# Output projection of a hybrid attention block: w_out loaded and split once per group, and the second half's parts made beside the first half's projection

## The chip, the cores and the metric

The kernel runs on one core of a Trainium2 chip. The core has engines that work on their own and wait for each other by semaphores: TensorE (PE in the profile; its weight loads are PEld), VectorE (DVE), ScalarE (ACT), GpSimd (POOL) and SyncE (SP), whose queue issues most of the DMAs. The metric is the time of one execution on the device in microseconds (us); lower is better.

## The reference

One layer of a decoder for 1024 tokens of width 1024, in float32:

```python
h    = rmsnorm(x, attn_norm_w)
proj = h @ w_in                      # 1024 x 3072: q, k, v of two groups of 8 heads, head size 64
o_dil = dilated_attention(rope(norm(qa)), rope(norm(ka)), va)   # group A: windows 128/512/2048, strides 1/4/16
o_sb  = stick_breaking(qs, ksb, vs)  # group B: sigmoid breaks, reversed cumulative product, strictly causal
mixed = concat(rmsnorm(o_dil, dil_out_norm_w), rmsnorm(o_sb, sb_out_norm_w))   # 1024 x (512 + 512)
x = x + mixed @ w_out                # w_out: 1024 x 1024
h = rmsnorm(x, ffn_norm_w)
x = x + (silu(h @ w_gate) * (h @ w_up)) @ w_down                # inner width 2816
```

The change concerns the line `x = x + mixed @ w_out` and what prepares it. In the kernel group A (dilated) is group 0 and group B (stick-breaking) is group 1. The factor 1/rms of a token is the same for all 512 columns of its group, so the kernel multiplies the group's output by the norm weights first, projects it, and multiplies the result by the factor while adding it to x.

## The kernel before, in words

**Products in three parts.** Each float32 matrix product is made of three faster ones: both operands are split into a high half (a copy on ACT into the reduced type) and a low half (the difference, on DVE or POOL), and `mm3` (lines 91 to 96) sums high x high, high x low and low x high. So each operand of a product costs one ACT pass and one DVE pass first.

**Stages.** First x is normalised and projected for the dilated group. Then eight head pairs follow one another: pairs 1 to 4 are the dilated heads (`attend_a`), pairs 5 to 8 the stick-breaking heads (`attend_b`). In a stick-breaking pair, for each block of 128 queries and each of two heads: scores on PE (L442 to L445, up to two chunks of 512 keys), two sigmoids on ACT per chunk (L564, tiles kp and pb), a scan over the keys on DVE (L567), a product (L568, on POOL for the first head and on DVE for the second), then transposes on PE (L586, tile pt), their evacuation on ACT (L588, tile th) and the product with v (L595, tile pv). After the eight pairs come the feed-forward layers, which are long rows of products from PE.

**The background.** While the pairs run, a generator, `ahead` (line 783), makes other work bit by bit: the projections of the stick-breaking heads, and then group 0's output projection. Every step of it yields a cost in units. The loop over pairs (lines 819 to 836) takes steps as long as the units spent are below a limit that grows with the pair's progress: at pair 8 the limit is 134 + 18 x f, with f the share of the pair that is done. It is only looked at where `attend_b` yields; in pair 8 these limits are 134.1, 134.4, 138.4, 138.8, 139.2, 140.0, 140.6, 141.3, 143.2, 144.0, 145.0 (the last score block), 147.9 and 152.0. What is left after that is traced behind the pair. Each piece of background work is held behind the score matmul that was traced last (`hold`, line 86, and `gate`), so it can't run earlier than that. The projections take 124.8 units, the parts of group 0's first half 0.8, so its output projection starts at 125.6; each of its eight products of 128 tokens by 512 columns takes 2.6 units, half of the tokens 20.8.

**The output projection.** It is made in four quarters (group g, half hf of the tokens: 512 each):
- `merge_parts` (line 745) goes through the four 128-column slices of a group's output: it loads the slice (`load_o`, line 699, from HBM into one of two staging tiles, tag qr), and `out_parts` (line 684) makes its high half on ACT (L688), its low half on DVE (L689), its square on ACT (L693, L696), and adds the squares up on POOL (L697). Four steps, 0.2 units each.
- `load_wout(g, dh)` (line 714) loads the 512 rows of w_out of group g and the left or right 512 columns (dh 0 or 1) in four pieces of 256 KB (L718, three raw tiles, tag wraw) and splits each: copy on ACT (L725), difference on DVE (L726). The left half of group 0 goes to the tiles of the projection weights, all others to tiles of the tags qs and kh, of which there are four each and of which each head pair uses two.
- `merge` (line 753) makes the factor from the summed squares (`out_rstd`, line 704) and then, for each column half and each 128 tokens, `wout` (line 732): twelve matmuls (L92, L95, L96, tile yo) and an addition on DVE (L741).

Group 0's first half is done in `ahead` beside pairs 7 and 8; its weights come in four calls, since the right half is loaded in the middle of the left half's products, and both are loaded again for the second half. Then the parts of the second half are made (146.4 to 147.2 units) and projected. Group 1 follows behind pair 8 (lines 840 to 848), its second half among the first norms of the feed-forward part (lines 882 to 887), with weights loaded anew.

**The order.** A planner at build time fixes the order in which each engine works: it simulates the program with its own durations and, where several instructions could go, takes the one traced earlier. `after` (line 81) adds an order without a wait between engines. The low halves of group 1's w_out and parts are tied behind the last product of the last pair (`last_mul`). On the chip each engine works through its fixed order; one that waits holds up all behind it. SP's queue of DMAs does so too.

Of the kernel before, what the change touches and what calls it, by code (L numbers as in the profile page):

```python
# [32 lines left out]
def f(ap):  # L33
    return ap.bitcast(F32)
# [3 lines left out]
def tile_hybrid_block(ctx, tc, x, attn_norm_w, w_in, q_norm_w, k_norm_w, dil_w, sb_w,  # L38
# [5 lines left out]
    def H(name, dtype=FR):  # L44
        return big.tile([128, 4, 512], dtype, tag="H", name=name, bufs=8)
# [35 lines left out]
    def after(i, first, why, cls=mybir.DependencyClass.NoSync):  # L81

        tc.add_manual_dep(i.ins, first.ins.name,
                          mybir.DependencyInfo(cls, mybir.DependencyReason.DATA), reason=why)
# [6 lines left out]
    def mm3(ps, a, b, first, last, held=False):  # L91
        i = nc.tensor.matmul(ps, a[0], b[0], start=first, stop=False)  # L92
        if first or held:
            hold(i)
        nc.tensor.matmul(ps, a[0], b[1], start=False, stop=False)  # L95
        return nc.tensor.matmul(ps, a[1], b[0], start=False, stop=last)  # L96
# [35 lines left out]
    def P4(name, tag="P"):  # L132
        return att.tile([128, 1024], F32, tag=tag, name=name, bufs={"P": 6, "G": 2, "E": 2, "M": 1}[tag])
# [66 lines left out]
    for tb in range(NT):  # L200
# [15 lines left out]
        t = att.tile([128, 512], F32, tag="rq", name="rq", bufs=2)  # L216
# [20 lines left out]
    for nm, w in (("q", q_norm_w), ("k", k_norm_w)):  # L237
        t = P4("rope" + nm, "E").rearrange("p (s t e) -> p s t e", s=2, t=NT)
# [67 lines left out]
    def project_ahead(i, which, spare=False):  # L306

        if which < 2:
            d = raws[i, which] = dram.tile([128, 1024], F32, name="raw%d%d" % (i, which))
            lows[i, which] = dram.tile([128, 1024], F32, name="low%d%d" % (i, which))  # L310

        def done(hf, p):
            c = slice(hf * 512, hf * 512 + 512)
            if which == 2:
                t = att.tile([128, 512], F32, tag="rq", name="rq", bufs=2)
                nc.scalar.activation(t, p, AF.Copy)
                turns.append(lambda: by_tokens(t, i, hf))
            else:
                h = att.tile([128, 512], FR, tag="rq", name="rh", bufs=2)
                l = att.tile([128, 512], FR, tag="rl", name="rl", bufs=3)  # L320
                split(h, l, p)
                nc.sync.dma_start(d[:, c], f(h))
                nc.sync.dma_start(lows[i, which][:, c], f(l))
                ready.add((i, which, hf))
        wt = weights(1536 + which * 512 + 128 * i, spare)
        return [project(wt, hf, done) for hf in range(2)]
# [357 lines left out]
    def out_parts(g, i, hf, o, parts, acc):  # L684

        w = ow[:, 4 * g + i:4 * g + i + 1]
        h, l = parts[hf][0][:, i, :], parts[hf][1][:, i, :]
        hold(nc.scalar.activation(h, o, AF.Copy, scale=w))  # L688
        j = nc.vector.scalar_tensor_tensor(l, o, w, f(h), op0=ALU.mult, op1=ALU.subtract)  # L689
        if g:  # L690
            after(j, last_mul[0], "the last pair goes first")
        if i == 0:
            hold(nc.scalar.activation(acc[hf], o, AF.Square))  # L693
        else:
            sq = att.tile([128, 512], F32, tag="rt", name="sq", bufs=3)
            hold(nc.scalar.activation(sq, o, AF.Square))  # L696
            nc.gpsimd.tensor_tensor(acc[hf], acc[hf], sq, op=ALU.add)  # L697

    def load_o(g, i, hf):
        t = att.tile([128, 512], F32, tag="qr", name="o", bufs=2)  # L700
        nc.sync.dma_start(t, (oa, ob)[g][i][:, hf * 512:hf * 512 + 512])
        return t

    def out_rstd(g, hf, acc):

        ssp = PS.tile([128, 4], F32, "d", "ssp")
        for k in range(4):
            nc.tensor.matmul(ssp[:, k:k + 1], acc[hf][:, k * 128:(k + 1) * 128], ones, start=True, stop=True)
        r = big.tile([128, 4], F32, name="rg%d%d" % (g, hf))
        nc.vector.tensor_scalar(r, ssp, 1.0 / 512, EPS, op0=ALU.mult, op1=ALU.add)  # L710
        nc.gpsimd.tensor_tensor(r, r, mhalf[:, :4], op=ALU.pow)
        return r

    def load_wout(g, dh):
        wts = []
        for i in range(4):
            raw = big.tile([128, 512], F32, tag="wraw", name="raw", bufs=3)
            nc.sync.dma_start(raw, w_out[g * 512 + i * 128:g * 512 + (i + 1) * 128, dh * 512:dh * 512 + 512])  # L718
            if g or dh:
                t = att.tile([128, 1024], FR, tag=("qs", "kh")[i // 2], name="wo", bufs=4)  # L720
                h, l = t[:, :512], t[:, 512:]
            else:

                h, l = ((att if i == 3 else big).tile([128, 512], FR, tag="rl" if i == 3 else tag, name="wo", bufs=3) for tag in ("wh", "wl"))
            nc.scalar.activation(h, raw, AF.Copy)  # L725
            j = nc.vector.tensor_tensor(l, raw, f(h), op=ALU.subtract)  # L726
            if g:
                after(j, last_mul[0], "the last pair goes first")
            wts.append((h, l))
        return wts  # L730

    def wout(tb, dh, r, parts, wts, tag):
        p = PS.tile([128, 512], F32, tag, "yo")
        c = slice((tb % 4) * 128, (tb % 4) * 128 + 128)
        for i in range(4):
            h, l = parts[tb // 4]
            mm3(p, (h[:, i, c], l[:, i, c]), wts[i], i == 0, i == 3, True)
            if i < 3:
                yield 0.65
        xx = x2[tb // 2][:, 2 * (tb % 2) + dh, :]  # L740
        nc.vector.scalar_tensor_tensor(xx, p, r[:, tb % 4:tb % 4 + 1], xx, op0=ALU.mult, op1=ALU.add)  # L741

    ahead_w = []

    def merge_parts(g, hf, parts, acc):
        o = load_o(g, 0, hf)
        for i in range(4):
            nxt = None if i == 3 else cur.ot[hf] if g and i == 2 else load_o(g, i + 1, hf)
            out_parts(g, i, hf, o, parts, acc)
            o = nxt  # L750
            yield 0.2

    def merge(g, hf, parts, acc):

        r = out_rstd(g, hf, acc)
        if g and hf:
            wts = [load_wout(g, dh) for dh in range(2)]
            for tb in range(4, 8):
                for dh in range(2):
                    for _ in wout(tb, dh, r, parts, wts[dh], ("d", "s")[tb % 2]):  # L760
                        pass
            return
        for dh in range(2):
            wts = ahead_w.pop() if ahead_w else load_wout(g, dh)
            for tb in range(4 * hf, 4 * hf + 4):
                yield from wout(tb, dh, r, parts, wts, "d")
                if g == 0 and tb % 4 == 1 and hf + dh < 2:
                    ahead_w.append(load_wout(g, 1 - dh))
                yield 0.65

    def merge_half(hf):
# [11 lines left out]
    def ahead():  # L783
        for i in range(3):
            for which in (1, 0, 2):
                for part in project_ahead(i, which):
                    yield from part
        for part in project_ahead(3, 1):
            yield from part

        q, v = project_ahead(3, 0), project_ahead(3, 2, True)
        yield from q[0]
        yield from v[0]
        parts, acc = [merge_half(0)], []
        acc.extend(att.tile([128, 512], F32, tag="acc", name="acc", bufs=2) for _ in range(2))
        yield from merge_parts(0, 0, parts, acc)
        yield from q[1]
        yield from v[1]
        while turns:
            turns.pop(0)()  # L800
        yield from merge(0, 0, parts, acc)
        parts.append(merge_half(1))
        yield from merge_parts(0, 1, parts, acc)
        yield from merge(0, 1, parts, acc)

    rest = ahead()
    spent = [0.0]

# [31 lines left out]
    parts = [[H("oh"), H("ol")] for hf in range(2)]  # L840
    acc = [att.tile([128, 512], F32, tag="acc", name="acc", bufs=2) for _ in range(2)]
    for _ in merge_parts(1, 0, parts, acc):
        pass
    for _ in merge(1, 0, parts, acc):
        pass
    parts_1 = merge_parts(1, 1, parts, acc)
    for _ in range(3):
# [18 lines left out]
    for key, tags in (("b11", "PPPP"), ("b21", "PPvv")):  # L866
        t = [att.tile([128, 2, 512], FR, tag=tag, name=key, bufs=BUFS[tag]) for tag in tags]
# [15 lines left out]
        norm2(tb)  # L883
    for _ in parts_1:
        pass
    for _ in merge(1, 1, parts, acc):
        pass
    st = [H("b12", F32), H("b22", F32)]
    for tb in range(4, 8):
# [60 lines left out]
    g = [None] * NF  # L950
# [131 lines left out]
    for k, ft in enumerate(range(NF - LATE, NF)):  # L1082
        r = room[k // 2] if k < 4 else None
# [28 lines left out]
    for hf in range(2):  # L1112
        for ft in list(range(HF, NF - LATE)) + list(range(12 - LATE, HF)):
            c = slice(512 * hf, 512 * hf + 512)
# [5 lines left out]
    for tag, n in (("k2", 2), ("k2", 2), ("kh", 4)):  # L1120
        t = att.tile([128, 1024], F32, tag=tag, name="lk", bufs=n)
# [134 lines left out]
```

## Time and profile before

| | |
|---|---|
| time, median of 3 runs | 1290.96 us (1290.93 to 1292.22) |
| the profiled execution | 1290.87 us, of which span 1288.7 us |
| mean granted clock of TensorE | 0.997 |
| PE busy | 1258.6 us, 98% of the span |
| DVE, ACT, POOL busy | 64%, 47%, 30% |
| bytes moved by DMA | 180.98 MB |
| products of the output projection (tile yo) | 384 matmuls, first start 469.6, last 631.0 us |
| loads and splits of w_out | 32 of each, copies from 441.6 to 611.2 us |
| pair 8's score matmuls | from about 491 to 533 us |

The profile names an instruction by its line, engine, operation and tiles (written <- read). The page gives totals; the same for chosen stretches are windows; the timeline lists instructions in order, equal neighbours merged into one row with their count, and in brackets how long the engine stood idle before a row and what ended that. Matmuls overlap each other a little, so durations of neighbours are longer than the distance of their starts.

### The profile page before, as it was taken

Reading aid. Unit: us, or ns where it says so; the run is one execution under the profiler, and the core shown is the slowest. Engines: PE = TensorE matmul, PEld = TensorE weight load, DVE = VectorE, ACT = ScalarE, POOL = GpSimd, SP = SyncE. Lnnn points to the kernel's source line nnn. Section 1 sums busy time; section 2 is a strip of 40 time slices with the busy share of each in tenths; the row PEclk is TensorE's granted clock in tenths of the full one; section 3 lists DMA queues with packets and bytes.
Section 4 is the critical chain, followed back from the end, with each engine's and each line's share of the span. In section 5 each row is a group of like instructions: output and inputs, shape, how many; then the busy total and the mean of one; then the engine's idle time right before and its main releaser. Section 6 shows DMA issues by size and latency. Waiting matters only on the chain.

```text
span 1288.7 us, 18344 instructions
## 1 busy us (share of the span) xinstructions
PE 1258.6 (98%) x6260; PEld 994.5 (77%) x6260; DVE 830.8 (64%) x1413; ACT 606.0 (47%) x1273; POOL 380.4 (30%) x346
## 2 busy tenths in 40 slices
PE   8999999999999999789999999999999999999998
PEld 6888887777767777568888888888888887878886
DVE  5334356655576867926797677665546876797686
ACT  5431267776686877825473222323332223434442
POOL 2488723353433421312112223212212321010000
PEclk9999999999999999999999999999999999999999
DMA  9633143556646552213256544323445458530352
GB/s 264 238 115 114 49 144 97 150 134 169 168 126 187 190 172 74 82 57 99 66 175 209 172 147 148 113 68 110 144 147 180 137 173 286 161 134 11 130 179 98
DMA packets 198029, 180.98 MB, mean 140 GB/s; under 512 B 33584, under 2 KB 142384, under 8 KB 197936
## 3 DMA queue, kind: packets, MB, share of 16 engines
q1 hardware_dynamic: 195760, 173.39, 43.6%
q0 software_dynamic: 2176, 6.42, 1.8%
q8 instruction: 49, 0.80, 0.3%
q14 instruction: 44, 0.36, 0.1%
HBM read 138.15 MB, written 41.62 MB: 139 GB/s over the span
## 4 chain that ended last, share of the span: by engine, by line
PE 84%; DMA 6%; DVE 4%; ACT 3%; issue 2%; POOL 1%; SPq 0%; DVEq 0%; POOLq 0%; ACTq 0%
PE yd L1156 14%; PE gu L95 11%; PE gu L96 11%; PE gu L92 11%; PE va L96 3%; PE va L92 3%; PE va L95 3%; PE pp L92 3%; PE pp L95 3%; PE pp L96 3%; PE pv L595 2%; PE yo L92 2%; PE yo L96 2%; PE yo L95 2%; PE pt L586 2%
## 5 line engine op out<-in xcount | busy, mean ns | idle before, releaser
L916 ACT ACTIVATE wh<-wr 128x512 fp32r<-128x512 f32 x132 | 83.4, 632 | 211.9 <-PE gu L95 171.7
L95 PE MATMUL gu<-t,wh 128*128 128x512 f32 x352 | 139.0, 395 | 0.0
L92 PE MATMUL gu<-t,wh 128*128 128x512 f32 x352 | 138.8, 394 | 0.0
L96 PE MATMUL gu<-t,wl 128*128 128x512 f32 x352 | 138.8, 394 | 0.0
L1156 PE MATMUL yd<-dl,dh 128*128 128x512 f32 x308 | 122.2, 397 | 2.4 <-DVE dl L917 1.4
L1156 PE MATMUL yd<-dh,dl 128*128 128x512 f32 x308 | 121.1, 393 | 0.0
L95 PE MATMUL gu<-b,wh 128*128 128x512 f32 x264 | 104.5, 396 | 0.0
L92 PE MATMUL gu<-b,wh 128*128 128x512 f32 x264 | 104.3, 396 | 0.0
L96 PE MATMUL gu<-b,wl 128*128 128x512 f32 x264 | 104.2, 396 | 0.0
L567 DVE TENSOR_TENSOR_SCAN kp<-kp,aside 128x640 f32<-128x640 f32 (+7 forms) x56 | 79.0, 1422 | 32.7 <-ACT kp L564 32.6
L1156 PE MATMUL yd<-dh 128*128 128x512 f32 x308 | 85.0, 395 | 0.0
L917 DVE TENSOR_TENSOR wl<-wr,wh 128x512 fp32r<-128x512 f32 x105 | 79.6, 758 | 7.8 <-ACT wh L916 7.8
L92 PEld LDWEIGHTS gu<-t,wh 128*128 128x128 f32 x352 | 66.2, 188 | 15.8
L95 PEld LDWEIGHTS gu<-t,wh 128*128 128x128 f32 x352 | 66.2, 188 | 15.7
L96 PEld LDWEIGHTS gu<-t,wl 128*128 128x128 f32 x352 | 66.1, 188 | 15.7
L92 PE MATMUL pp<-hh,wh 128*128 128x512 f32 x192 | 78.0, 406 | 0.0
L916 ACT ACTIVATE dh<-wd 128x512 fp32r<-128x512 f32 x55 | 34.8, 632 | 89.9 <-PE yd L1156 81.6
L92 PE MATMUL va<-wt,hh 128*128 128x512 f32 x192 | 76.4, 401 | 0.6 <-ACT hh L63 0.5
L96 PE MATMUL va<-wt,hl 128*128 128x512 f32 x192 | 75.9, 398 | 0.9 <-DVE hl L64 0.7
L95 PE MATMUL va<-wt,hh 128*128 128x512 f32 x192 | 75.7, 397 | 0.2 <-DVE wt L154 0.2
L96 PE MATMUL pp<-hh,wl 128*128 128x512 f32 x192 | 75.6, 394 | 0.0
L95 PE MATMUL pp<-hl,wh 128*128 128x512 f32 x192 | 75.6, 394 | 0.0
(216 smaller groups left out, 3025.4 us busy)
## 6 DMA issues: line engine op xcount, KB each, us to landing
wd<-in_w_down_dram SPq DMA_DIRECT2D x88, 256.0 KB, 2.8
wr<-in_w_gate_dram SPq DMA_DIRECT2D x80, 256.0 KB, 3.0
wr<-in_w_up_dram SPq DMA_DIRECT2D x60, 256.0 KB, 3.0
raw<-in_w_in_dram SPq DMA_DIRECT2D x48, 256.0 KB, 4.7
raw<-in_w_out_dram SPq DMA_DIRECT2D x32, 256.0 KB, 2.7
g<-gu SPq DMA_DIRECT2D x20, 256.0 KB, 5.4
xt<-in_x_dram SPq DMA_DIRECT2D x8, 512.0 KB, 7.1
qk<-qr SPq DMA_DIRECT2D x16, 256.0 KB, 2.0
```

The costliest lines, as they stand in the source:

```text
L92: i = nc.tensor.matmul(ps, a[0], b[0], start=first, stop=False)
L95: nc.tensor.matmul(ps, a[0], b[1], start=False, stop=False)
L96: return nc.tensor.matmul(ps, a[1], b[0], start=False, stop=last)
L567: nc.vector.tensor_tensor_scan(rv, rv, (aside[0] if aside[0] is not None else zero)[:, 0:1].to_broadcast([128, n]), 1.0, op0=ALU.mult, op1 ...
L586: i = nc.tensor.transpose(pt[:, c:c + 128], pq[k][s][:, j * 128:(j + 1) * 128], ident)
L595: i = nc.tensor.matmul(pr.pv[64 * s:64 * s + 64, c - n:c], pr.v[:, j, 64 * s:64 * s + 64], th[:, n * s:n * s + n], start=j == 0, stop=j == ...
L916: nc.scalar.activation(h, r, AF.Copy)
L917: i = two(n).tensor_tensor(l, r, f(h), op=ALU.subtract)
L1156: mm = nc.tensor.matmul(pp[k], a[x][:, c], b[y], start=not more and j == order[0] and x + y == 0, stop=j == order[-1] and x == 1, skip_gro ...
```

## The change

`load_wout` becomes a generator: it traces one of its four pieces at each step and hands out the list of tiles, which grows. Both column halves of group 0 are loaded once, ahead of the first half's products: the left half whole and the first piece of the right; the other pieces of the right are traced one after each of the left half's four products. The tiles are kept for the second half of the tokens. In the same way one step of `merge_parts(0, 1)` is traced after each of the first half's four products of the right columns. For group 1 both column halves are loaded ahead of its first half's products and kept for its second half. The x tiles and part tiles of group 0's second half (`merge_half(1)`) are allocated ahead of the first half's products.

```diff
     def load_wout(g, dh):
         wts = []
         for i in range(4):
...
             wts.append((h, l))
-        return wts
+            yield wts
...
-    ahead_w = []
-
...
+    def step(*others):
+
+        for t in others:
+            next(t, None)
+
-    def merge(g, hf, parts, acc):
+    def merge(g, hf, parts, acc, wts, beside=None):
 
         r = out_rstd(g, hf, acc)
         if g and hf:
-            wts = [load_wout(g, dh) for dh in range(2)]
             for tb in range(4, 8):
                 for dh in range(2):
                     for _ in wout(tb, dh, r, parts, wts[dh], ("d", "s")[tb % 2]):
                         pass
             return
         for dh in range(2):
-            wts = ahead_w.pop() if ahead_w else load_wout(g, dh)
             for tb in range(4 * hf, 4 * hf + 4):
-                yield from wout(tb, dh, r, parts, wts, "d")
-                if g == 0 and tb % 4 == 1 and hf + dh < 2:
-                    ahead_w.append(load_wout(g, 1 - dh))
+                yield from wout(tb, dh, r, parts, wts[dh], "d")
+                if beside is not None:
+                    step(beside[dh])
                 yield 0.65
...
-        yield from merge(0, 0, parts, acc)
+        loads = [load_wout(0, dh) for dh in range(2)]
+        wts = [next(t) for t in loads]
+        for _ in loads[0]:
+            pass
         parts.append(merge_half(1))
-        yield from merge_parts(0, 1, parts, acc)
-        yield from merge(0, 1, parts, acc)
+        yield from merge(0, 0, parts, acc, wts, (loads[1], merge_parts(0, 1, parts, acc)))
+        yield from merge(0, 1, parts, acc, wts)
...
-    for _ in merge(1, 0, parts, acc):
+    loads = [load_wout(1, dh) for dh in range(2)]
+    wts = [[a, b, c, d][-1] for a, b, c, d in loads]
+    for _ in merge(1, 0, parts, acc, wts):
         pass
...
-    for _ in merge(1, 1, parts, acc):
+    for _ in merge(1, 1, parts, acc, wts):
         pass
```

The number of matmuls doesn't change. The four steps of `merge_parts(0, 1)` no longer count in the background's units, so the second half's projection starts at 146.4 units instead of 147.2; the steps themselves fall at 137.95, 140.55, 143.15 and 145.75.

## The prediction

> **What bounds the kernel now.** The page's first part comes first, then the same table by windows. In the windows the columns are stretch and length, then busy time with instruction count of PE, its weight loads, DVE, ACT and POOL, then granted clock, DMA share and GB/s.
>
> ```profile
> PE 1258.6 (98%) x6260; PEld 994.5 (77%) x6260; DVE 830.8 (64%) x1413; ACT 606.0 (47%) x1273; POOL 380.4 (30%) x346
> ```
>
> ```profile
> 500.00:520.00 20.00, 20.00 (x143) 14.50 (x142) 11.94 (x13) 14.98 (x34) 3.27 (x3) 1.00 0.13 41
> 520.00:535.00 15.00, 14.61 (x81) 10.61 (x81) 13.56 (x11) 13.05 (x30) 3.32 (x2) 1.00 0.15 51
> 535.00:540.00 5.00, 2.49 (x17) 1.36 (x15) 4.95 (x5) 5.00 (x11) 4.23 (x2) 1.00 0.44 138
> 540.00:545.00 5.00, 1.06 (x4) 0.66 (x5) 4.90 (x4) 3.64 (x7) 2.60 (x2) 0.69 0.40 130
> 545.00:550.00 5.00, 5.00 (x26) 3.46 (x25) 3.88 (x6) 1.35 (x4) 0.14 (x1) 0.63 0.71 224
> 550.00:555.00 5.00, 4.53 (x27) 3.11 (x26) 1.57 (x3) 2.86 (x6) 2.23 (x2) 1.00 0.55 199
> 555.00:560.00 5.00, 2.11 (x10) 1.37 (x8) 1.41 (x2) 3.17 (x7) 2.90 (x4) 1.00 0.16 54
> 560.00:565.00 5.00, 4.87 (x27) 3.58 (x28) 0.75 (x1) 1.44 (x4) 0.94 (x1) 1.00 0.00 0
> 565.00:660.00 95.00, 94.94 (x454) 77.34 (x453) 65.30 (x100) 44.76 (x85) 15.86 (x23) 1.00 0.25 78
> ```
>
> TensorE is busy for 98% of the span, so work taken from another engine is worth nothing wherever PE stays full. The change touches 440 to 631 us. There PE is full up to 520 and again from 565 on, and idle in one place: between 535 and 565 its busy times add to 20.06 of 30 us, 9.94 us idle, and for ten of them the clock is below full. I call this hole the tail: the end of the eighth head pair. What the change is worth has to come from there. The timeline of PE shows what each gap waited for (in brackets: idle before the row, and its releaser):
>
> ```profile
> 526.79 1.03 PE L586 MATMUL pt<-ident,pb 128*128 128x128 f32 x8
> 527.75 1.08 PE L595 MATMUL pv<-th,v 128*64 128x256 f32 x8
> ...
> 532.72 0.50 PE L442 MATMUL sc<-kh,qs 128*128 128x512 f32 x1 [0.36 <-ACT pb L564]
> ...
> 537.71 0.66 PE L586 MATMUL pt<-ident,pb 128*128 128x128 f32 x4 [0.87 <-POOL pb L568]
> 543.47 0.69 PE L586 MATMUL pt<-ident,pb 128*128 128x128 f32 x2 [5.11 <-DVE pb L568]
> 544.63 1.97 PE L586 MATMUL pt<-ident,pb 128*128 128x128 f32 x8 [0.47 <-ACT th L588]
> 546.53 1.98 PE L595 MATMUL pv<-th,v 128*64 128x256 f32 x8
> ...
> 552.23 0.66 PE L586 MATMUL pt<-ident,pb 128*128 128x128 f32 x4 [0.47 <-ACT th L588]
> ...
> 560.13 0.93 PE L586 MATMUL pt<-ident,pb 128*128 128x128 f32 x6 [3.02 <-ACT th L588]
> ```
>
> The gaps are 0.87, 5.11, 0.47, 0.47 and 3.02 us, together 9.94. The largest waits for the last product of the second head (L568 on DVE). Now the two engines that feed it, ACT and then DVE:
>
> ```profile
> 534.20 0.81 ACT L688 ACTIVATE oh<-o,ow 128x512 fp32r<-128x512 f32 x1
> 534.82 0.72 ACT L693 ACTIVATE acc<-o 128x512 f32<-128x512 f32 x1
> 535.34 0.81 ACT L688 ACTIVATE oh<-o,ow 128x512 fp32r<-128x512 f32 x1
> 535.95 0.71 ACT L696 ACTIVATE sq<-o 128x512 f32<-128x512 f32 x1
> 536.47 0.71 ACT L725 ACTIVATE wo<-raw 128x512 fp32r<-128x512 f32 x1
> 536.99 0.67 ACT L564 ACTIVATE kp<-sc 128x512 f32<-128x512 f32 x1
> ...
> 537.95 1.24 ACT L725 ACTIVATE wo<-raw 128x512 fp32r<-128x512 f32 x2
> ...
> 558.96 0.63 ACT L696 ACTIVATE sq<-o 128x512 f32<-128x512 f32 x1 [1.83 <-DMA o<-ob]
> 559.50 1.07 ACT L588 ACTIVATE th<-pt 128x512 f32<-128x512 f32 x2
> ```
>
> ```profile
> 532.65 2.28 DVE L567 TENSOR_TENSOR_SCAN kp<-kp,aside 128x1024 f32<-128x1024 f32 x1
> 535.05 0.75 DVE L689 SCALAR_TENSOR_TENSOR ol<-o,ow,oh 128x512 fp32r<-128x512 f32 x1
> 535.72 0.74 DVE L741 SCALAR_TENSOR_TENSOR x<-yo,rg,x 128x512 f32<-128x512 f32 x1
> 536.38 1.82 DVE L689 SCALAR_TENSOR_TENSOR ol<-o,ow,oh 128x512 fp32r<-128x512 f32 x1
> 538.12 1.76 DVE L726 TENSOR_TENSOR wo<-raw,wo 128x512 fp32r<-128x512 f32 x1
> 539.81 2.27 DVE L567 TENSOR_TENSOR_SCAN kp<-kp,aside 128x1024 f32<-128x1024 f32 x1
> 542.18 1.23 DVE L568 TENSOR_TENSOR pb<-pb,kp 128x1023 f32<-128x1023 f32 x1
> ```
>
> The last score chunk is on PE at 532.72. On ACT five pieces of output work come before its kp, from 534.20 to 536.99: two parts of the dilated second half with their squares, and a copy of w_out. DVE ends its first scan at about 534.9 and starts the second at 539.81, with two low halves, one addition and one w_out split between. So the hole is made by the very work that the change moves or removes, and PE has no other products there, because the second half's projection waits for the same parts.
>
> **The change part by part.** *Loads and splits.* w_out is loaded in 256 KB pieces, 32 before (the page's raw<-in_w_out_dram row) and 16 after: four calls of four pieces instead of eight.
>
> ```profile
> L725 ACT ACTIVATE wo<-raw x32: 615/634/724, 441.6 to 611.2; 128x512 fp32r<-128x512 f32 x32
> L726 DVE TENSOR_TENSOR wo<-raw,wo x32: 654/684/2157, 444.6 to 612.6; 128x512 fp32r<-128x512 f32 x32
> ```
>
> That removes 16 copies of 0.634 us on ACT (10.1 us) and 16 splits of 0.684 us on DVE (10.9 us). Of the four removed calls, the second load of (group 0, left) stood at about 492 to 500, inside full PE: worth 0. The two of group 1's second half stood at 591 to 612, inside the stretch in which PE has 94.94 of 95 us: 0, covered by the projection itself. Only the second load of (group 0, right), at 528 to 538, stands in the tail. Its last copy (536.47) and split (538.12) are two of the intruders; it is priced below with them.
>
> Two rows for the next point, from DVE and from ACT: a projection tile's addition every 0.75 + 2.06 = 2.81 us, and the copies of group 1's right half.
>
> ```profile
> 575.41 0.75 DVE L741 SCALAR_TENSOR_TENSOR x<-yo,rg,x 128x512 f32<-128x512 f32 x1 [2.06 <-PE yo L96]
> ```
>
> ```profile
> 578.92 2.03 ACT L725 ACTIVATE wo<-raw 128x512 fp32r<-128x512 f32 x3 [11.50 <-PE yo L96]
> ```
>
> *The tiles that are held longer.* Both right-column loads use the four tiles that head pairs use. Pair 8 has taken its own two of each tag before the first call, and group 0's right load waits for pair 7's scores as before. Group 1's right load took its tiles at 578.9 us, when PE finished the last left-over product of group 0, and will again; its user comes four products (4 x 2.81 = 11 us) later. Price 0; without that cover it is that wait, a rival below.
>
> *The parts moved.* By the background's budget (the section on the kernel has its numbers) the dilated second half starts at 146.4 units, so all four of its steps are traced at the yield of pair 8 with limit 147.9, held behind the last score matmul: that is the 534.20 above. After, the steps fall at 137.95, 140.55, 143.15 and 145.75, so at the yields with limits 138.4, 140.6, 143.2 and 147.9. Three steps go to about 495 to 525, and only the fourth stays behind the last score. Moved with each step: two ACT passes, one DVE low half, one POOL addition and the next load on SP. There PE has 20.00 of 20 us, DVE 8 and ACT 5 us free: 0 as long as pair 8's own chain has slack there, and as a bound 3 x (0.81 + 0.72) on ACT + 3 x 0.75 on DVE = 6.8 us if none.
>
> *What that gives the tail.* (1) With one step instead of two and no w_out copy, ACT's last kp starts near 535.3 at worst (534.20 plus the 1.14 us between rows 534.20 and 535.34), and the second scan near 536 to 537 instead of 539.81: 3 to 4 us earlier. The rest of the 5.11 us can be filled by products of the second half, of which three quarters can now run, 2.81 us a tile. I take all 5.11; the bounds are 0 and 5.11. (2) Without that gap the clock doesn't fall: eight transposes took 1.97 us instead of 1.03 and eight pv products 1.98 instead of 1.08. That is 0.94 + 0.90 = 1.84 us; bounds 0 and 1.84, I take 1.8. (3) The 0.87 us wait on POOL: half, 0.4. (4) The gaps 0.47, 0.47 and 3.02 us wait for ACT, which stood behind a load of the other group's output (558.96). Those loads can start earlier, since the two staging tiles come free earlier, but the order is still planned and ACT still works in order: bounds 0 and 3.96, I take 1.5. (5) New friction in pair 8, between 0 and the 6.8 above: 0.6, near the low end, since PE was full there with DVE 40% free.
>
> On (2), the Trainium skill, "TensorE: Matmul & The Clock Gate", Part 1, says that PE falls to half clock after about 3.4 us without work and needs as much busy time to come back. The trace agrees: the gap of 5.11 us is followed by 0.63, the gap of 3.02 us leaves 1.00. By that rule a remnant under 3.4 us would cost no clock, which is the 1.8 I took.
>
> Sum: 5.1 + 1.8 + 0.4 + 1.5 - 0.6 = 8.2 us. The profiled execution took 1290.87 us (span 1288.7 and 2.2 around it), 0.09 under the median of the runs. 1290.87 - 8.2 = 1282.7; on the median, **1282.8**. From 565 us on PE is full, so the gain should arrive whole at the end.
>
> **The rivals.** *A, the hole is filled with other work (0.16).* The planner orders each engine by its own durations. With staging tiles free, group 1's copies and squares can slide in front of the last kp, five passes again. For it: in the old order group 1's first copies stand right behind it, at 537.95. Against: group 1's DVE halves are tied behind the last L568, so only ACT is delayed. The 5.11 us gap then stays near 3.5 us, the clock is mostly saved, nothing else is: 1290.9 - 1.6 - 1.4 = 1287.9.
>
> *B, the change doesn't do what it says (0.10).* The parts are ready, but PE's order keeps the transposes in front, and ACT, 13.05 of 15 us busy from 520 and 5.00 of 5 from 535, is itself the limit. Then the hole moves and hardly shrinks: 1290.9 - 1 = 1289.9.
>
> The row for rival C, the POOL additions:
>
> ```profile
> L697 POOL TENSOR_TENSOR acc<-acc,sq x12: 1262/1295/1727, 440.6 to 589.0; 128x512 f32<-128x512 f32 x12
> ```
>
> *C, slower (0.10).* The moved steps wait in ACT's queue of pair 8. Each of its last two needs a load that is issued only when a staging tile is free, and ACT stood 1.83 us before such a load at 558.96. Behind it stand the sigmoids and evacuations that PE needs. Two such waits, 3.7 us, the 6.8 us bound of the passes, and three POOL additions of 1.30 us that hold up DVE passes, 3.9 us, are 14.4 us; against a tail that still gains the 5.1 + 1.8 this is 1290.9 + 14.4 - 6.9 = 1298.4 in full. It decides once the new waits cost more than 6.9 us, and at 10 us, which I take for its time, it gives 1294.
>
> For this last price speaks the Trainium skill, "SBUF — State Buffer", section "SBUF: two separate sides": a DVE instruction with two SBUF inputs and a reading POOL instruction block each other for a whole instruction. The 1.82 us of the low half at 536.38 against 0.75 at 535.05 agrees with it.
>
> **How the numbers follow.** The forecast has 0.64, A 0.16, B 0.10, C 0.10. A measurement of this kernel can tell 0.2%, 2.6 us, from no change: faster means below 1288.4. The forecast's own range: all gaps and the clock back, 9.94 + 1.84 = 11.8, gives 1279.1, and with the 0.39 us that PE stood idle from 520 to 535 1278.7; I open it at 1278. With (1) at 3.5 and (4) at 0 it is 1290.9 - 5.1 = 1285.8. To leave out no more than 0.2, the range goes up over A: 1278 to 1288.8. Faster: 0.64 + 0.12 of A = 0.76. Same: 0.04 of A, 0.09 of B, 0.01 of C = 0.14. Slower: 0.09 of C and 0.01 of B = 0.10.
>
> **What would show it.** In the changed profile: 16 loads, copies and splits of w_out; three low halves of the dilated second half before the last score matmul, one behind it; no PE wait over 3.4 us for DVE L568 and a granted clock of 1.00 throughout the eighth pair's end; second-half products between the last transposes; PE idle between the last scores and the feed-forward part down from 9.9 to 2 to 4 us. I am wrong if the tail shrinks and the time doesn't (then something after 565 took it back), if the gap keeps its size behind other passes (A), or if new gaps stand in front of score matmuls or evacuations of pair 8 (C).

## The result, and the profile after

| | before | changed |
|---|---|---|
| time, median | 1290.95 us (4 runs, 1289.17 to 1292.22) | 1282.38 us (4 runs, 1279.39 to 1283.76) |
| ratio | | 0.9932, 95% interval 0.9909 to 0.9954 |
| profiled execution | 1290.87 us, span 1288.7 | 1283.40 us, span 1281.6 |

The change is 0.68% faster, 8.6 us by the medians; 1282.8 was forecast. The page's first line of the changed kernel, then its windows (columns as in the prediction):

```profile
PE 1256.7 (98%) x6260; PEld 995.1 (78%) x6260; DVE 824.9 (64%) x1397; ACT 596.3 (47%) x1257; POOL 381.2 (30%) x346
```

```profile
500.00:520.00 20.00, 20.00 (x136) 14.79 (x135) 11.59 (x14) 13.82 (x31) 4.88 (x5) 1.00 0.12 40
520.00:530.00 10.00, 9.23 (x53) 7.04 (x52) 8.91 (x8) 8.81 (x20) 3.35 (x3) 1.00 0.09 28
...
540.00:545.00 5.00, 4.16 (x22) 3.35 (x22) 4.90 (x4) 1.92 (x4) 1.98 (x2) 1.00 0.42 157
545.00:550.00 5.00, 3.31 (x16) 2.60 (x17) 4.63 (x9) 2.74 (x6) 1.84 (x2) 1.00 0.64 201
...
565.00:660.00 95.00, 95.00 (x454) 77.47 (x453) 66.60 (x102) 45.34 (x87) 16.81 (x23) 1.00 0.24 73
```

That last stretch is as full as before, and the clock is 1.00 in all of them in this execution (two later profiles of the same kernel differ, see "The change again"). For the whole tail, 535 to 565 us, one window row each, first of the kernel before and then of the changed one:

```profile
535.00:565.00 30.00, 20.07 (x106) 13.55 (x105) 17.47 (x19) 17.46 (x33) 13.04 (x9) 0.89 0.38 124
```

```profile
535.00:565.00 30.00, 27.17 (x148) 20.20 (x147) 19.04 (x19) 14.36 (x27) 10.27 (x7) 1.00 0.27 88
```

The tail's idle time on PE fell from 9.93 to 2.83 us. PE's busy time over the whole span, with the same 6260 matmuls, is 1.9 us shorter. That is not yet the price of the low clock in the tail, because PE waits and its clock falls in other places too; it is taken below from the stretch that the change touches. What PE does in the old gap now:

```profile
538.84 0.87 PE L586 MATMUL pt<-ident,pb 128*128 128x128 f32 x5
540.74 1.05 PE L708 MATMUL ssp<-ones,acc 128*128 128x1 f32 x8 [1.03 <-POOL acc L697]
541.65 0.48 PE L92 MATMUL yo<-wo,oh 128*128 128x512 f32 x1
...
544.51 0.38 PE L586 MATMUL pt<-ident,pb 128*128 128x128 f32 x2
545.53 0.66 PE L586 MATMUL pt<-ident,pb 128*128 128x128 f32 x4 [0.64 <-ACT th L588]
547.35 0.50 PE L92 MATMUL yo<-wo,oh 128*128 128x512 f32 x1 [1.16 <-DVE rg L710]
```

Between the transposes that stood 5.11 us apart there is now a whole projection tile of the second half, 541.65 to 544.5. The transposes at 544.51 don't wait any more. Two short waits are new: for the sum of squares (1.03) and for the second half's factor (1.16). ACT and DVE show why the wait for L568 would not be gone without those products:

```profile
516.15 0.75 ACT L688 ACTIVATE oh<-o,ow 128x512 fp32r<-128x512 f32 x1
...
532.74 1.28 ACT L726 ACTIVATE wo<-raw 128x512 fp32r<-128x512 f32 x2
...
536.43 0.91 ACT L688 ACTIVATE oh<-o,ow 128x512 fp32r<-128x512 f32 x1
537.04 0.81 ACT L696 ACTIVATE sq<-o 128x512 f32<-128x512 f32 x1
537.56 0.80 ACT L726 ACTIVATE wo<-raw 128x512 fp32r<-128x512 f32 x1
538.08 0.77 ACT L564 ACTIVATE kp<-sc 128x512 f32<-128x512 f32 x1
```

```profile
534.54 2.29 DVE L567 TENSOR_TENSOR_SCAN kp<-kp,aside 128x1024 f32<-128x1024 f32 x1 [0.57 <-ACT kp L564]
537.37 2.17 DVE L689 SCALAR_TENSOR_TENSOR ol<-o,ow,oh 128x512 fp32r<-128x512 f32 x1 [0.54 <-ACT oh L688]
539.47 0.74 DVE L742 SCALAR_TENSOR_TENSOR x<-yo,rg,x 128x512 f32<-128x512 f32 x1
540.13 2.27 DVE L567 TENSOR_TENSOR_SCAN kp<-kp,aside 128x1024 f32<-128x1024 f32 x1
542.50 1.22 DVE L568 TENSOR_TENSOR pb<-pb,kp 128x1023 f32<-128x1023 f32 x1
```

The steps did move (their low halves start at 498.1, 517.1 and 523.4 us), and the fourth stayed in the tail. But copies of w_out still stand in front of the last kp, now those of group 1 (532.74 and 537.56). The last product starts at 542.50.

Two executions can't be laid side by side by the time axis alone. Pair 8 itself begins at another time in each (its first product on POOL, in the timeline of before and then of the change):

```profile
495.31 0.69 POOL L568 TENSOR_TENSOR pb<-pb,kp 128x127 f32<-128x127 f32 x1 [5.62 <-ACT kp L564]
```

```profile
497.64 0.41 POOL L568 TENSOR_TENSOR pb<-pb,kp 128x127 f32<-128x127 f32 x1 [5.62 <-ACT kp L564]
```

So the last L568 starts 46.9 us after that point before (542.18) and 44.9 after: 2.0 us sooner. The last addition of the output projection starts at 631.5 us before and 623.9 after, which makes the *stretch* from pair 8's first product to it 136.2 and 126.3 us. I use the stretch below, because it leaves out what happens ahead of pair 8; what follows it takes 656.0 to 658.6 us in every profile of this study. As windows, before and then changed:

```profile
495.31:631.47 136.16, 125.78 (x661) 96.32 (x661) 88.56 (x117) 74.20 (x154) 32.06 (x33) 0.97 0.24 78
```

```profile
497.64:623.93 126.29, 122.69 (x661) 95.20 (x661) 80.24 (x101) 65.07 (x137) 33.10 (x33) 1.00 0.16 51
```

With the same 661 matmuls, PE is busy 3.1 us less, which goes with the clock, and idle 6.8 us less (10.38 and 3.60). Together that is the whole 9.9 us.

### The profile page after: what moved, and what is told of

The parts are those of the page before. It is cut to its first block, busy times and chain, and to the rows that moved or that the text cites. A ratio compares the mean times of both kernels' runs of the same rounds, so it can differ in the third digit from the quotient of the medians.

```text
span 1281.6 us, 18256 instructions
## 1 busy us (share of the span) xinstructions
PE 1256.7 (98%) x6260; PEld 995.1 (78%) x6260; DVE 824.9 (64%) x1397; ACT 596.3 (47%) x1257; POOL 381.2 (30%) x346
## 4 chain that ended last, share of the span: by engine, by line
PE 87%; DMA 4%; DVE 4%; ACT 2%; issue 1%; POOL 1%; SPq 0%; DVEq 0%; POOLq 0%; ACTq 0%
PE yd L1163 13%; PE gu L95 11%; PE gu L96 11%; PE gu L92 11%; PE va L96 3%; PE va L92 3%; PE va L95 3%; PE pp L92 3%; PE pp L95 3%; PE pp L96 3%; PE pv L595 2%; PE pt L586 2%; PE yo L92 2%; PE pv L519 2%; PE yo L96 2%; PE yo L95 2%
```

## The experiments

The theory: the gain is the closing of the hole in the tail, because the second half's parts are early, so that PE has products there and less stands in front of the last scan. The rivals: it is the work saved (16 copies, splits and loads), or other work takes the place on ACT (rival A).

| kernel | ratio to before, 95% interval | median us | stretch us |
|---|---|---|---|
| before | | 1289.96 to 1290.63 | 136.2 |
| the change, again | 0.9932 (0.9908 to 0.9955) | 1282.15 | 126.4 |
| the change, a third time | 0.9933 (0.9911 to 0.9955) | 1282.82 | 126.4 |
| weights once, alone | 0.9979 (0.9963 to 0.9995) | 1287.44 | 134.8 |
| parts beside, alone | 0.9934 (0.9909 to 0.9958) | 1282.14 | 126.8 |
| group 1's weights once, alone | 1.0006 (0.9989 to 1.0023) | 1291.17 | 138.3 |
| change, no products in the tail | 0.9959 (0.9943 to 0.9976) | 1285.41 | 130.2 |
| before, with dummy matmuls in the gap | 0.9973 (0.9955 to 0.9992) | 1286.69 | 131.0 |
| change, group 1 behind the last sigmoid | 0.9896 (0.9876 to 0.9916) | 1276.64 | 123.5 |
| the same again | 0.9902 (0.9884 to 0.9921) | 1279.55 | 123.5 |
| change, parts still earlier | 0.9914 (0.9897 to 0.9931) | 1279.97 | 125.3 |
| both of these | 0.9905 (0.9888 to 0.9923) | 1278.81 | 123.3 |
| before, group 1 behind the last sigmoid | 0.9995 (0.9979 to 1.0012) | 1290.13 | 137.8 |

The median of before differs by chip. The stretch is of one profile of each kernel and has a spread of its own: the last row's kernel turns out to have the order of before on every engine, so 136.2 and 137.8 are two executions of the same work, and the kernel with 138.3 differs from before only behind the tail. The three profiles of the change agree within 0.2 us.

**Weights once, alone.**

```diff
-        yield from merge(0, 0, parts, acc, wts, (loads[1], merge_parts(0, 1, parts, acc)))
+        yield from merge(0, 0, parts, acc, wts, (loads[1], iter(())))
+        yield from merge_parts(0, 1, parts, acc)
         yield from merge(0, 1, parts, acc, wts)
```

> The weights half alone: w_out is loaded and split once per group, and the four steps for the second half's parts stay between the halves as before. Theory (the hole in the tail closes because the parts are there early, so PE has products): only the copy and split of group 0's second right load leave the tail, so about 2 of the 8.6 us come, near 1289, and a PE wait of 3 us or more for DVE L568 stays. Rival (the gain is the work saved on ACT, DVE and the DMA queues): most of it comes, 1284 or less.

Measured 0.9979: 2.5 us by the medians (the interval allows 0.6 to 4.8). The gap is still there. PE and then ACT of this kernel:

```profile
543.77 0.69 PE L586 MATMUL pt<-ident,pb 128*128 128x128 f32 x2 [5.10 <-DVE pb L568]
```

```profile
535.52 0.78 ACT L688 ACTIVATE oh<-o,ow 128x512 fp32r<-128x512 f32 x1
536.14 0.69 ACT L693 ACTIVATE acc<-o 128x512 f32<-128x512 f32 x1
536.66 0.77 ACT L688 ACTIVATE oh<-o,ow 128x512 fp32r<-128x512 f32 x1
537.27 0.68 ACT L696 ACTIVATE sq<-o 128x512 f32<-128x512 f32 x1
537.79 0.68 ACT L726 ACTIVATE wo<-raw 128x512 fp32r<-128x512 f32 x1
538.31 0.65 ACT L564 ACTIVATE kp<-sc 128x512 f32<-128x512 f32 x1
```

Five passes stand in front of the last kp, as before. The load that was saved left a place, and group 1's load took it. That is rival A's mechanism, seen in this half of the change. What this half does gain lies beside the gap: PE's wait of 0.87 us for POOL is gone, and those for evacuations fell from 3.96 to 1.73 us. Part of that is lost again to the clock, which is low for longer here (0.50 in the windows 545 to 550 and 550 to 555).

**Parts beside, alone.** The kernel before, with `merge_half(1)` ahead of the first half's products and one step after each right product:

```diff
                 if g == 0 and tb % 4 == 1 and hf + dh < 2:
                     ahead_w.append(load_wout(g, 1 - dh))
+                if beside is not None and dh:
+                    next(beside, None)
...
-        yield from merge(0, 0, parts, acc)
         parts.append(merge_half(1))
-        yield from merge_parts(0, 1, parts, acc)
+        yield from merge(0, 0, parts, acc, merge_parts(0, 1, parts, acc))
```

> The other half alone: the second half's four steps beside the first half's right products, with w_out loaded as often as before. Theory: most of the gain, 6 to 8 us, near 1284, and PE's tail idle falls from 9.9 to about 4 us; the second right load still delays ACT and DVE there. Rival (saved work): less than 2 us, above 1289.

Measured 0.9934, the whole gain. Its tail:

```profile
535.00:565.00 30.00, 28.66 (x149) 21.55 (x149) 19.39 (x20) 15.86 (x30) 10.53 (x7) 0.94 0.33 114
```

1.34 us idle, although the second right load is still made. The saved work is not needed for the gain: with none of it saved, nothing measurable is lost. The clock falls here, to 0.74 in the window from 540 to 545, and the gain is whole all the same.

**Group 1's weights once, alone.**

```diff
-    for _ in merge(1, 0, parts, acc):
+    once = [load_wout(1, dh) for dh in range(2)]
+    for _ in merge(1, 0, parts, acc, once):
...
-    for _ in merge(1, 1, parts, acc):
+    for _ in merge(1, 1, parts, acc, once):
```

> Before, with only group 1's weights kept for its second half (8 copies and 8 splits less, all behind pair 8). Theory: PE is full there, so no gain, within 1 us of before. Rival (saved work): up to 8 x 0.68 us of DVE, 2 to 5 us faster.

Measured 1.0006: no difference, as expected, with eight loads, copies and splits less.

**The change again.** No edit.

> The changed kernel once more, on the same chip as its parts, as the common measure. Both theories: 0.993 of before. Also asked: whether pair 8 starts about 2 us later than before again, as in the first profile, or whether that belongs to one execution; I expect the latter.

Measured 0.9932. Pair 8's first product starts at 494.1 us here, 3.5 us earlier than in the first profile of the same kernel. So the 2.3 us by which it was late there belong to that execution.

So does the clock of 1.00. In this profile it is 0.81 and 0.85 in the windows from 535 to 545, and in the third profile of the change (the last run below) 0.66 in one of them:

```profile
540.00:545.00 5.00, 5.00 (x20) 3.99 (x19) 4.90 (x5) 1.24 (x2) 1.56 (x1) 0.66 0.35 120
```

```profile
496.44:622.86 126.42, 123.98 (x661) 96.30 (x661) 80.46 (x100) 65.12 (x137) 33.42 (x33) 0.99 0.16 51
```

In this third profile PE is busy 1.3 us longer in the stretch than in the first and idle 1.2 us less (2.44 for 3.60): the wait of 1.16 us for the factor doesn't occur. The stretch is 126.4 in both later profiles and 126.3 in the first. So it isn't a clock of 1.00 that makes the change fast; the slower matmuls took time in which PE would have waited.

**No products in the tail.** The background stops ahead of the second half's projection, which is then held behind the last pv product:

```diff
-            while spent[0] < LEAD + sum(RATES[:n]) + RATES[n] * done / 24.0:
+            while spent[0] < min(146.0, LEAD + sum(RATES[:n]) + RATES[n] * done / 24.0):
...
+    gate[0] = last_pv[0]
     while spent[0] < 1000:
         more()
```

> The changed kernel, but the second half's products are held behind the last pv product of pair 8, so PE has none of them in the tail; the parts are as early as in the change. It tells the two halves of step (1) apart. Theory now, after the profiles (the gap is filled with products; the chain to the last L568 got only some 2 us shorter): the wait for DVE L568 comes back with 3 to 4 us, PE idles 8 us or more in the tail, and 5 us or more of the 8 are lost: 1287 to 1291. Rival (the shorter chain is the gain, as half of my step had it): 1285 or less.

Measured 0.9959, 1285.4 us, between the two expectations. Without products the stretch is 3.9 us longer than with them (130.2 against 126.3), and still 6.0 shorter than before. PE, then two windows:

```profile
544.51 0.89 PE L586 MATMUL pt<-ident,pb 128*128 128x128 f32 x5
546.41 1.36 PE L710 MATMUL ssp<-ones,acc 128*128 128x1 f32 x8 [1.01 <-POOL acc L699]
549.47 0.69 PE L586 MATMUL pt<-ident,pb 128*128 128x128 f32 x2 [1.71 <-DVE pb L568]
550.70 1.97 PE L586 MATMUL pt<-ident,pb 128*128 128x128 f32 x8 [0.53 <-ACT th L588]
...
556.70 0.92 PE L586 MATMUL pt<-ident,pb 128*128 128x128 f32 x6 [0.40 <-ACT th L588]
...
559.88 0.87 PE L595 MATMUL pv<-th,v 128*64 128x256 f32 x8 [1.24 <-ACT th L588]
```

```profile
545.00:550.00 5.00, 2.28 (x14) 1.72 (x12) 4.90 (x5) 2.50 (x5) 2.16 (x2) 0.70 0.47 157
550.00:555.00 5.00, 4.47 (x24) 3.14 (x24) 4.65 (x8) 3.40 (x6) 1.99 (x2) 0.62 0.44 142
```

From 545.40 to 549.47 PE has only the eight one-column products of the sum: the wait for the last L568 is 4.1 us, in pieces, where it was 5.11, and the low clock is back. Of the 6.0 us, 3.3 are the waits up to the last L568 (0.87 + 5.11 before, 1.01 + 1.71 here, with the products of the sum now standing inside the gap) and 1.8 those for evacuations behind it (0.47 + 0.47 + 3.02 = 3.96 before, 0.53 + 0.40 + 1.24 = 2.17 here). The other 0.9 is PE's busy time in the stretch, 1.3 us shorter than before, less a new wait of 0.45 us ahead of the tail. So the earlier parts alone bring more than half, by a shorter chain, work for PE inside the gap and less in front of the evacuations, and the products close what is left. Neither expectation holds as a whole. This kernel has an order of its own behind the gap, so the 1.8 us need not be the change's share.

**Dummy matmuls in the gap.** The kernel before, with 48 matmuls whose result nobody reads:

```diff
+    wp = PS.tile([128, 512], F32, "s", "fill")
+    for _ in range(48):
+        w = nc.tensor.matmul(wp[:, :128], ident_r, strict, start=True, stop=True)
+        after(w, behind, "between the transposes")
     i = transpose()
+    after(i, w, "between the transposes")
```

> Before, with 48 matmuls of 128 columns that nobody reads put on PE between the last block's third and fourth transposes, where the 5.11 us gap is. It measures the clock by itself: no useful work moves, only the gap is no gap for the clock. Theory: granted clock 1.00 throughout, the eight transposes at 1.03 instead of 1.97 us, 1 to 2 us faster than before. Rival (the low clock cost nothing, since PE then waits for ACT anyway): no change, 1290.

Measured 0.9973: 3.9 us by the medians, above the 1 to 2 us of the theory, but the interval allows 1.0 to 5.8. PE:

```profile
537.82 5.56 PE L1263 MATMUL fill<-strict,ident_r 128*128 128x128 f32 x48
...
545.26 1.14 PE L586 MATMUL pt<-ident,pb 128*128 128x128 f32 x8 [1.43 <-ACT th L588]
546.33 1.08 PE L595 MATMUL pv<-th,v 128*64 128x256 f32 x8
```

The clock stays at 1.00; the eight transposes take 1.14 us instead of 1.97 and the eight pv products 1.08 instead of 1.98, 1.7 us together. The rest is not the clock alone: with the dummies the planner also ordered the evacuations behind the gap differently, and the wait of 3.02 us is gone. As a measure of the clock alone the run is therefore only good for those two rows, and by itself it doesn't exclude the rival.

**Group 1 behind the last sigmoid.** The change, with `last_sig` the last L564, and this at group 1's w_out copies, high halves and first square:

```diff
+            if g:
+                after(c, last_sig[0], "the last pair goes first")
```

> The changed kernel with group 1's ACT passes (copies of w_out, high halves, squares) ordered behind the last sigmoid of pair 8, as their DVE passes are already. Theory: three copies of w_out leave the path to the last kp, which starts 1 to 1.5 us earlier; PE is filled by products, so the time gains 0 to 1 us against the change: 1281 to 1282. Rival A (other work on ACT holds what is left of the tail): 2 us or more, 1280 or less.

> The changed kernel with group 1's ACT passes behind the last sigmoid once more, on the same chip as the change: it gained 5 us on the change between two calls, while its profile is only 2.9 us shorter from the eighth pair to the last projection. I expect 2 to 4 us.

Measured 0.9896 and 0.9902: by the ratios some 5 and 4 us better than the change, and 3.3 us by the medians of the one chip on which both ran. The intervals of the second run and of the change overlap; the stretch tells them apart, 123.5 in both profiles against 126.3 to 126.4 in three. So it is 2.7 to 2.9 us, more than the theory said, and rival A was at work inside the change. The last kp has two passes in front of it instead of three after the last evacuation, no copies of w_out stand between the kps before, and the two new waits of PE shrink; its waits from 485 to 680 us, in the second of these runs:

```profile
PE pt L586 <- DVE pb L568: 1.5, 2, 1.0
PE sc L442 <- ACT pb L564: 0.7, 2, 0.3
PE ssp L714 <- POOL acc L703: 0.2, 1, 0.2
PE yo L92 <- DVE rg L716: 0.2, 1, 0.2
```

**Parts still earlier.** The four steps beside the third and fourth left product and the first and second right one.

```diff
-        yield from merge(0, 0, parts, acc, wts, (loads[1], merge_parts(0, 1, parts, acc)))
+        w, m = loads[1], merge_parts(0, 1, parts, acc)
+        yield from merge(0, 0, parts, acc, wts, [(w,), (w,), (w, m), (m,), (m,), (m,), (), ()])
```

> The changed kernel with the four steps two products earlier: beside the first half's third and fourth left products and first and second right ones, so that all four are behind scores of pair 8's first five blocks and none behind its last. Theory: the waits of PE for the sum of squares (1.03) and for the factor (1.16) and the fourth low half before the last scan go; 1 to 2 us under the change, 1280 to 1281. Rival C (steps in pair 8 make new waits there): slower than the change.

Measured 0.9914, 1280.0 us, as expected, though the interval overlaps that of the change. The stretch is 1.0 us shorter, but that flatters it: a moved step now runs ahead of pair 8's first product, which starts 8.22 us after pair 7's last one (496.07 and 487.85) instead of 7.63 in the change. From pair 7's last product on, the gain is only 0.4 us. PE in pair 8:

```profile
500.81 0.50 PE L92 MATMUL yo<-wo,oh 128*128 128x512 f32 x1 [1.13 <-DVE x L742]
...
504.81 1.14 PE L586 MATMUL pt<-ident,pb 128*128 128x128 f32 x8 [1.15 <-ACT th L588]
```

The change has neither of these two waits, nor a third for an addition, 1.06 us at 547.11. What the theory named is gone (the waits for the sum and for the factor, and the fourth low half before the last scan), but rival C's new waits did come and took back most of what that gave, without making the kernel slower.

**Both.**

> The changed kernel with both: group 1's ACT passes behind the last sigmoid, and the four steps two products earlier. Theory (what is left in the tail is ACT and DVE work in front of the last kp and scan): now nothing of the output stands there, the last scan starts right behind the first, 1 to 2 us under the kernel with the order alone, 1275 to 1276. Rival (the tail is full of products already): the same as with the order alone.

Measured 0.9905. The scans of this kernel stand one behind the other, with nothing of the output between them:

```profile
532.90 2.29 DVE L567 TENSOR_TENSOR_SCAN kp<-kp,aside 128x1024 f32<-128x1024 f32 x1 [0.85 <-ACT kp L564]
535.90 2.29 DVE L567 TENSOR_TENSOR_SCAN kp<-kp,aside 128x1024 f32<-128x1024 f32 x1 [0.71 <-ACT kp L564]
```

The last scan starts 39.8 us after pair 8's first product (535.90 - 496.10) instead of 42.5 in the change. But the time is that of the order alone, so here the rival was right. With the order alone PE idled only 0.40 of the 30 us from 535 to 565, so a still shorter chain had next to nothing to close, and the earlier steps bring one of their own waits in pair 8 again (1.14 us at 500.85).

**The order alone, on the kernel before.**

> Before, with only the order of group 1's ACT passes behind the last sigmoid. Theory: in the kernel before, what stood in front of the last kp were the dilated second half's steps and group 0's w_out copies, none of group 1's, and PE had no products: at most 2 us faster, 1288 to 1291. Rival A (group 1's passes are what holds the tail): 4 us or more.

Measured 0.9995: nothing, as the theory said. But this run could not have shown anything else. In the two profiles PE, ACT, DVE and POOL work through the same instructions in the same order from the first to the last: the planner had put group 1's passes behind the last sigmoid already (the first is the copy at 537.95 us), so the edit moved nothing. The run is a second measurement of the kernel before. What it does show is that on the kernel before no pass of group 1 stood in the way; group 0's did.

> The changed kernel as the measure for the three others: 0.993 of before, near 1282.

Measured 0.9933. The best version is the change with group 1's ACT passes behind the last sigmoid, 0.9902 (0.9884 to 0.9921) on the same chip as this third run of the change; with the steps also earlier it is the same within the intervals.

## Why the prediction was right, step by step

- **The bound.** Right: the hole between 535 and 565 us is where the time came from. What lies behind the projection takes 657.2 us before and 657.7 in the change.
- **Loads and splits at 0.** Right for group 1 (1.0006). For group 0's right load the reasoning was off: I counted its copy and split among the intruders that would go. Alone, the saving brings about 2.5 us and leaves the 5.10 us gap, because group 1's load slides into its place.
- **Term (1), 5.1 us.** The size was near: of the gap only the 1.03 us wait for the sum of squares is left, 4.1 us gained. The working was not: I had the last scan 3 to 4 us earlier; it came 2.0 us earlier (the last L568 44.9 instead of 46.9 us after pair 8's first product), since the fourth step and group 1's copies stayed in front. Products did more of it than I had said.
- **Term (2), 1.8 us.** Too small, and its reason holds only in part. Over the stretch PE's busy time for the same matmuls fell by 3.1 us in the first pair of profiles; the two rows that the term adds up make 1.84 of that, but the clock was low from 541.9 to 548.7 us, over more rows than these (the prediction's ten us are two windows, each low for a part). And "without that gap the clock doesn't fall" failed in two of the three profiles of the change: there busy time fell by only 1.8 us, idle time by 7.9, and the stretch came out the same. So the terms for the clock and for the gaps can't be counted apart, and the sign "a granted clock of 1.00 throughout" came true in one execution out of three.
- **Term (3), 0.4 us.** The 0.87 us wait for POOL is gone whole.
- **Term (4), 1.5 us.** Of 3.96 us, 0.64 are left, so 3.3 were gained; the new wait for the factor gives 1.16 back. Net 2.2.
- **Term (5), 0.6 us.** From 520 to 535 us PE now idles 0.77 us where it idled 0.39: 0.4.
- The terms as measured in the first pair of profiles: 4.1 + 3.1 + 0.9 + 2.2 - 0.4 = 9.9 us, the whole shortening of the stretch, against a forecast of 8.2. The first term was too large, the others too small, and the friction was feared more than it cost. What follows the stretch is 0.5 us longer in that profile, which leaves 9.4 from pair 8's first product to the end (793.4 and 784.0). The time fell by 8.6 us by the medians, with an interval of 6 to 12. So the mechanism and the size are right, and that the forecast lies 0.4 us from the median is luck.
- **Rival A** was not a rival but a part: its passes came, without taking the gain, since PE had products. They cost about 3 us, which the order shows. **B** didn't happen. **C** stayed at the 0.4 us of term (5) in the change; with the steps moved still earlier its waits came.

## What to carry to other kernels

An in-order engine's tail is made by what stands in front of the late instruction, so removing one such piece can do nothing if the planner has another ready to put in its place: weights loaded once brought about 2.5 us alone and nothing measurable on top of the parts, and only with the change, which let group 1's passes into the tail, is their order worth about 3 us. Before an order is tested on a second kernel, see whether it moves anything there. What closes a wait on the bounding engine is independent work that is ready by then; look for what that work itself waits for and make it earlier. And compare the stretch that the change touches, from one common instruction to another, not the absolute times of two profiles; take the first one ahead of everything that the edit moves, and take more than one profile before a clock of 1.00 is put down to the change.

## What was not expected of the hardware

- **The clock falls without a long gap.** In the kernel without products PE's longest gap from 545.40 to 549.47 is 1.71 us, with eight one-column products in the 4.1 us; the clock is 0.70 and 0.62 in the two windows around and behind it. The Trainium skill, "TensorE: Matmul & The Clock Gate", Part 1, speaks of a window of about 3.4 us and of how busy PE was in it. The 5.11 us gap before agrees; this run adds that single gaps, which I had used as the measure in the prediction, are not what counts. The change shows the same: its clock stays at 1.00 in the profile with gaps of 1.03, 0.64 and 1.16 us and falls to 0.66 behind the gap of 1.02 us in another. And where a wait of 3.02 us left 1.00 in the profile before, one of 2.67 us at the same place is followed by 0.77 in the second measurement of that order. What decides in waits of 1 to 3 us is not shown; one profile doesn't tell.
- **The program ahead of the change varies by more than the change is worth.** Pair 8's first product starts between 494.1 and 503.3 us in these profiles, and in the change the order of PE's instructions is that of before up to there. Runs of the change spread by 5 us on one chip (1278.4 to 1283.5) and by 9 on another (1279.0 to 1288.0). It goes with the clock ahead of pair 8: the start is 494.1 to 496.6 us where the clock stays at 1.00 from the first 10 us up to there, 496.1 to 497.6 with one fall, 499.1 and 499.4 with two, and 503.3 with three. In all of these but one the first fall stands at about 246 us, behind a wait of PE for a DVE result (tile st, L463): 2.31 us in the first profile of the change, 0.45 in the second, whose clock stays at 1.00 there. Why that wait varies is not shown.
- **A low half takes three times as long beside POOL.** L689 on DVE takes 0.74 us in the change where nothing runs on POOL (498.12) and 2.17 in the row at 537.37, which starts while POOL's product of the first head is running (the row below, of the changed kernel). The prediction had 1.82 for the same pair of operations.

```profile
537.00 2.00 POOL L568 TENSOR_TENSOR pb<-pb,kp 128x1023 f32<-128x1023 f32 x1 [4.92 <-DVE kp L567]
```
